# A one-core decoder step: two one-word loads at the start, four token blocks in two transfers, the sample store on another queue

## Chip, core and metric

The kernel runs on one core of a Trainium2 chip. The metric is the device time of one execution in microseconds, as the median of several runs. Engines are called as the profile calls them or by their names: PE or TensorE (matrix products), DVE or VectorE, ACT or ScalarE, POOL or GpSimd, SP or SyncE (which here issues loads and stores).

## The reference

One inference step of a decoder trunk with two parallel head groups: 1024 new prompt tokens and 32 sample tokens (8 sequences of 4), model width 1024, all in float32.

```python
h = rmsnorm(x, norm_g)
proj = h @ w_in                       # 1024 -> 3584: q, f, i (V), za, glu, zb
...
o_a, s_new = hgrn2_chunked(q, k, v, logf, s0)
o_a = rmsnorm(o_a, a_norm_g) * silu(za)
u = glu[..., :B] * sigmoid(glu[..., B:])
cv, buf_new = causal_dwconv(u, conv_buf, conv_w, conv_b)
o_b = silu(layernorm(cv, ln_g, ln_b)) * silu(zb)
out = concat([o_a, o_b]) @ w_out
...
y = rmsnorm(x + out, final_norm_g)    # prompt and sample tokens
```

The outputs are y for both kinds of tokens and the new recurrent and convolution states.

## The kernel before

Tokens lie in nine blocks: eight of 128 prompt tokens (0 to 7) and one of the 32 sample tokens (8). `program` (L1301) emits the kernel twice through `emit`: once in a fast form, then, under a branch on a flag that the fast form has computed, once in a slow form that is safe for extreme inputs. With these inputs the branch is taken over the slow form, so every engine jumps over its instructions at the end.

The start of `emit`. ScalarE loads an activation table (L239). TensorE does 13 products on a constant tile that only keep it busy (`keep(NWARM)`, L245). SP issues the loads in a written order: block 0 (L154), the weights `gin` of the first norm, one row for all 128 partitions (L249), the first of four slices of V's columns of `w_in` (`wi`, L254), block 1, the other three slices, then blocks 2, 8, 3, 4, 5, 6, 7. Blocks 4 to 7 go into `cv`, a tile that is free at that time, one transfer each. After that come the small constants, `cols` (L342) first.

For each block, `stats_x` (L174) has ScalarE square and sum a row, take logarithm and exponential for the root (L176 to L178), and VectorE multiply the block with the root and `gin`. `turn_x` (L193) transposes the block on TensorE, and ScalarE and VectorE split it into a high and a low part. V of blocks 0 and 1 is multiplied slice by slice (`v_part`), with products that only keep TensorE busy in between. `seq` fixes the order of these instructions on each engine as they are written.

Then come 28 blocks of `w_in`'s columns, the recurrence, the convolution and the output product, all woven together by a scheduler. Each load or store carries one of eight completion semaphores in turn (DMAHW0 to DMAHW7), and its issue waits for the transfer that had this semaphore before.

The end. `sample_out` (L1180) follows the last prompt block: TensorE multiplies the 32 sample tokens, VectorE adds the input, ScalarE squares and sums, TensorE adds up over partitions with a matrix of ones (`bones`, L1201), VectorE and ScalarE make the root with one correction step, VectorE multiplies result, root and the final norm's weights `gs` in one instruction, and SP stores it:

```python
V.scalar_tensor_tensor(ys, ys, y, gs, ALU.mult, ALU.mult)
nc.sync.dma_start(h["o_ys"], ys)
```

Behind it `program` loads the flag into a register of every engine (L1305) and branches (L1306); then all engines meet at the barrier that ends the program (L1394).

Of the kernel before, what the change touches and what calls it, by code (L numbers as in the profile page):

```python
# [14 lines left out]
AF = mybir.ActivationFunctionType  # L15
ALU = mybir.AluOpType
AX = mybir.AxisListType

P = 128
D = 1024  # L20
# [12 lines left out]
EPS = 1e-6  # L33
# [20 lines left out]
C_END = C_LOG + 8  # L54
# [43 lines left out]
def emit(nc, tc, h, fast, flag_out=None):  # L98
    HW = 5
    with ExitStack() as ctx:  # L100
# [5 lines left out]
        def sb(shape, tag, bufs=1, dt=F32):  # L106
            return pool.tile(shape, dt, tag=tag, name=tag, bufs=bufs)

        def big(dt=F32, w=TOK):
            return pool.tile([P, 4, w], dt, tag="big", name="big", bufs=6)  # L110

        def bank(tag, bufs):
            return psp.tile([P, 512], F32, tag=tag, name=tag, bufs=bufs)
# [4 lines left out]
        def aux():  # L118
            return bank("aux", 2)

        S = nc.scalar
        V, T = Clock(nc.vector, _dve_ns), Clock(nc.tensor, _pe_ns)
# [17 lines left out]
        gin = sb([P, D], "u", 2)  # L140
        cv = big()
# [4 lines left out]
        X = {"raw": 1, "u": 2, "wh": 2, "qkg": 5}  # L146
        XTAG = ("raw", "u", "wh", "wh", "raw", "qkg", "u", "wh", "qkg")

        def load_x(tb):
            n = P if tb < 8 else ST  # L150

            xr = cv[:, tb - 4, 0:D] if 4 <= tb < 8 else sb([P, D], XTAG[tb], X[XTAG[tb]])
            src = h["xp"][tb * P : (tb + 1) * P, :] if tb < 8 else h["xs"]
            nc.sync.dma_start(xr[0:n, :], src)  # L154
            return xr, n

        def after(ins, prev):
            tc.add_manual_dep(
                getattr(ins, "ins", ins),
                getattr(prev, "ins", prev).name,  # L160
                mybir.DependencyInfo(mybir.DependencyClass.NoSync, mybir.DependencyReason.DATA),
                reason="order of one engine",
            )
# [78 lines left out]
        def keep(n, rhs=av):  # L242

            for _ in range(n):
                seq("P", T.matmul(warm[:, 0:P], lhsT=av, rhs=rhs, start=True, stop=True))  # L245

        keep(NWARM)
        xs = {0: load_x(0)}
        nc.sync.dma_start(gin, h["gin"].partition_broadcast(P))  # L249
        keep(2, gin[:, 0:P])  # L250
        wrs = []
        for j in range(4):
            wr = sb([P, 2, 512], "wraw" if j < 2 else "wl", 2)
            nc.sync.dma_start(wr, h["wi"][:, 2 * j : 2 * j + 2, :])  # L254
            wrs.append(wr)
            if j == 0:
                xs[1] = load_x(1)
        for tb in (2, 8, 3, 4, 5, 6, 7):
            xs[tb] = load_x(tb)


        v01 = [bank("ops", 1), bank("ptps", 1)]
# [75 lines left out]
        S.copy(vs, vps[:, 0:P])  # L338


        cols = sb([P, C_END], "cols")
        nc.sync.dma_start(cols, h["cols"])  # L342
        nmask = 1 if fast else NMASK
        masks = sb([P, nmask, P], "masks", dt=U8)
# [24 lines left out]
        bones = sb([P, P], "bones")  # L369
# [627 lines left out]
        for i, (kind, c) in enumerate(order):  # L997
# [10 lines left out]
            w = ws.pop(0)  # L1008
# [27 lines left out]
            elif kind == "f":  # L1036
# [7 lines left out]
                for hf in range(4):  # L1044
                    gs = g[:, hf * 256 : hf * 256 + 256]
                    V.tensor_tensor_scan(gs, rst, gs, 0.0, ALU.mult, ALU.add)
                gs = g[:, SEQ:TOK]
# [64 lines left out]
        for ko in range(KO):  # L1112
# [17 lines left out]
            ins = S.copy(hi, wr)  # L1130
# [50 lines left out]
        def sample_out(prev):  # L1181
            ys, gs = sio
            ops_s = bank("ops", 1)
            for ko in range(KO):
                for q in range(4):
                    ins = T.matmul(
                        ops_s[q * ST : (q + 1) * ST, 0:256],
                        lhsT=(mixa if ko < 4 else cv)[:, ko % 4, SEQ:TOK],
                        rhs=wraws[ko][:, q * 256 : (q + 1) * 256],
                        start=(ko == 0),  # L1190
                        stop=(ko == KO - 1),
                        tile_position=(0, q * ST),
                    )
                    after(ins, prev)
                    prev = ins
            V.tensor_tensor(ys, ops_s[:, 0:256], ys, ALU.add)
            sq = sb([P, 1], "ss", 4)
            junk = sb([P, 512], "ho", 2)
            S.activation(junk[:, 0:256], ys, AF.Square, accum_out=sq)  # L1199
            sp = aux()  # L1200
            T.matmul(sp[:, 0:1], lhsT=bones, rhs=sq, start=True, stop=True)  # L1201
            y = sb([P, 1], "ss", 4)
            w = sb([P, 1], "ss", 4)

            V.tensor_scalar(w, sp[:, 0:1], -0.5 / D, -0.5 * EPS, ALU.mult, ALU.add)
            S.activation(y, sp[:, 0:1], AF.Ln, bias=eps, scale=1.0 / D)  # L1206
            S.activation(y, y, AF.Exp, scale=-0.5)  # L1207
            V.scalar_tensor_tensor(w, y, y, w, ALU.mult, ALU.mult)
            V.scalar_tensor_tensor(y, w, 1.5, y, ALU.add, ALU.mult)
            V.scalar_tensor_tensor(ys, ys, y, gs, ALU.mult, ALU.mult)  # L1210
            nc.sync.dma_start(h["o_ys"], ys)

        def split_mix(tb):
            ts = slice(tb * P, (tb + 1) * P)
# [10 lines left out]
        def out_mm(ps, mix, half, ko):  # L1225
            hi, lo = mix
            whi, wlo = wo[ko]
            for j, (a, w) in enumerate(
                ((hi, whi[:, half * 512 : half * 512 + 512]), (hi, wlo[half]),
                 (lo, whi[:, half * 512 : half * 512 + 512]))  # L1230
            ):
                ins = T.matmul(
                    ps,
                    lhsT=a[:, ko, :],
                    rhs=w,
                    start=(ko == 0 and j == 0),
                    stop=(ko == KO - 1 and j == 2),
                )
            return ins
# [49 lines left out]
        for tb in range(2, 8):  # L1289
# [3 lines left out]
            for half in range(2):  # L1293
                for ko in range(KO):
                    last = out_mm(ps[half], mix, half, ko)
            finish(tb, ps)
        sample_out(last)


def program(nc, tc, h, fallback=True):  # L1300
    with tc.tile_pool(name="flag", bufs=1) as fp:  # L1301
        flag = fp.tile([1, 1], I32, name="flag")
        emit(nc, tc, h, True, flag)
        if fallback:
            slow = nc.values_load(flag[0:1, 0:1], min_val=0, max_val=1)  # L1305
            with tc.If(slow > 0):  # L1306
                emit(nc, tc, h, False)

# [97 lines left out]
```

## Time and profile before

| | |
|---|---|
| median of 3 runs | 488.61 us (488.42 to 488.77) |
| profiled execution | 488.44 us |
| its span, first to last instruction | 486.7 us |
| TensorE busy | 477.5 us (98% of the span) |
| VectorE busy | 353.7 us (73%) |
| ScalarE busy | 258.3 us (53%) |
| mean granted TensorE clock | 0.994 |
| moved by DMA | 43.78 MB |

The profile is of one execution. Busy time counts an engine's instructions, but not loads of registers, branches, semaphore waits or the issuing of transfers. The time outside the span, 1.7 us here, is in the device time and not in the profile.

### The profile page before, as it was taken

What the parts mean: (1) busy time and instruction counts of PE and PEld (TensorE: products, weight loads), DVE (VectorE), ACT (ScalarE), POOL (GpSimd) and SP (SyncE); (2) the same over time, 40 slices, a digit from 0 to 9 for tenths busy, and PEclk for the clock granted to TensorE, in tenths of its full rate; (3) what the DMA queues carried; (4) which work ended last, traced back from release to release, by engine and by line L of the source; (5) the groups of instructions that cost most, each with busy time, mean ns of one, the idle gap of its engine ahead of it and who ended that gap; (6) DMA issues with size and microseconds to landing.
All of it is one profiled execution on the core that took longest, in us unless ns stands there. A gap on an engine that the chain in (4) does not pass through costs nothing.

```text
span 486.7 us, 7566 instructions
## 1 busy us (share of the span) xinstructions
PE 477.5 (98%) x2970; PEld 445.7 (92%) x2970; DVE 353.7 (73%) x670; ACT 258.3 (53%) x481; POOL 3.0 (1%) x20
## 2 busy tenths in 40 slices
PE   8999999999999999999999999999999999999993
PEld 7788899999999999999999999999999988888881
DVE  4764313999999988999699999995587767334322
ACT  5764322422686564563656547464877876333322
POOL 1000000000000000000000000000000000000000
PEclk9999999999999999999999999999999999999997
DMA  7910501221111202231121211131115289233111
GB/s 268 332 45 13 179 0 48 52 54 44 43 45 43 55 7 65 85 97 43 44 66 45 88 45 48 50 129 46 45 50 172 78 302 386 79 114 145 43 44 61
DMA packets 23628, 43.78 MB, mean 90 GB/s; under 512 B 10881, under 2 KB 12673, under 8 KB 23457
## 3 DMA queue, kind: packets, MB, share of 16 engines
q1 hardware_dynamic: 22432, 41.13, 26.1%
q10 hardware_dynamic: 1152, 2.10, 1.1%
q8 instruction: 25, 0.41, 0.3%
q14 instruction: 19, 0.15, 0.1%
HBM read 35.72 MB, written 7.24 MB: 88 GB/s over the span
## 4 chain that ended last, share of the span: by engine, by line
PE 97%; DMA 1%; DVE 0%; ACT 0%; issue 0%; SPq 0%
PE mm L73 77%; PE ops L73 9%; PE ptps L73 7%; PE aux L73 5%; DMA u<-gin 1%; DVE ho L73 0%; DVE ss L73 0%; ACT ho L1199 0%; SPq L154 0%; ACT ss L1206 0%; ACT ss L1207 0%
## 5 line engine op out<-in xcount | busy, mean ns | idle before, releaser
L73 PE MATMUL mm<-big,wh 128*128 128x352 f32 (+1 forms) x1280 | 324.0, 332 | 0.0
L73 PEld LDWEIGHTS mm<-big,wh 128*128 128x128 f32 x1280 | 224.2, 188 | 6.7 <-issue 0.6
L73 PE MATMUL mm<-big,wl 128*128 128x352 f32 (+1 forms) x640 | 211.3, 330 | 0.0
L73 PEld LDWEIGHTS mm<-big,wl 128*128 128x128 f32 x640 | 120.5, 188 | 3.2
L73 DVE TENSOR_TENSOR wl<-wraw,wh 128x1024 fp32r<-128x1024 f32 x24 | 29.3, 1219 | 23.3 <-ACT wh L412 23.3
L73 DVE SCALAR_TENSOR_TENSOR big<-u,wsum,big 128x511 f32<-128x511 f32 (+14 forms) x60 | 44.3, 738 | 0.5
L73 DVE SCALAR_TENSOR_TENSOR big<-u,cols,big 128x511 f32<-128x511 f32 (+14 forms) x60 | 44.0, 735 | 0.0
L73 DVE SCALAR_TENSOR_TENSOR cq<-u,cols,cq 128x511 f32<-128x511 f32 (+13 forms) x56 | 41.1, 735 | 0.1
L73 DVE TENSOR_TENSOR qkg<-mm,big 128x512 f32<-128x512 f32 x16 | 11.0, 690 | 36.0 <-PE mm L73 28.7
L412 ACT CAST wh<-wraw 128x1024 fp32r<-128x1024 f32 x24 | 25.2, 1049 | 17.4 <-issue 7.8
L1259 ACT ACTIVATE big<-qkg 128x512 f32<-128x512 f32 x16 | 10.1, 631 | 35.8 <-DVE qkg L73 32.9
L417 ACT ACT_TABLE_LOAD x20 | 25.7, 1283 | 0.3
L480 ACT ACTIVATE qkg<-mm 128x352 f32<-128x352 f32 x48 | 19.4, 466 | 11.4 <-PE mm L73 11.3
L73 PE MATMUL mm<-vt,wh 128*128 128x512 f32 x64 | 25.0, 391 | 0.0
L73 PE MATMUL mm<-vt,wl 128*128 128x512 f32 x64 | 24.8, 390 | 0.0
L73 PE MATMUL ops<-big 128*128 128x512 f32 (+1 forms) x96 | 22.7, 395 | 0.0
L73 PE MATMUL ptps<-big 128*128 128x512 f32 x64 | 20.2, 396 | 0.0
L480 ACT ACT_TABLE_LOAD x15 | 19.2, 1283 | 0.3
L554 ACT ACTIVATE hw<-qkg,rng 128x128 f32<-128x128 f32 x32 | 10.2, 393 | 13.5 <-PE ops L73 13.5
L910 ACT ACTIVATE u<-mm,cols 128x352 f32<-128x352 f32 (+2 forms) x16 | 6.5, 485 | 17.7 <-PE mm L73 17.7
L73 PE MATMUL mm<-hw,wh 128*128 128x512 f32 x40 | 15.6, 389 | 0.0
L73 PEld LDWEIGHTS ops<-big 128*128 128x128 f32 (+1 forms) x96 | 12.6, 162 | 3.1 <-ACT big L284 0.2
(237 smaller groups left out, 637.1 us busy)
## 6 DMA issues: line engine op xcount, KB each, us to landing
wraw<-win SPq DMA_DIRECT2D x24, 512.0 KB, 3.6
wraw<-wo SPq DMA_DIRECT2D x8, 512.0 KB, 4.0
big<-xp SPq DMA_DIRECT2D x2, 2048.0 KB, 8.9
big<-xp SPq DMA_DIRECT2D x4, 512.0 KB, 11.1
raw<-sh SPq DMA_DIRECT2D x4, 512.0 KB, 3.4
o_hs<-raw SPq DMA_DIRECT2D x4, 512.0 KB, 2.9
o_yp<-qkg SPq DMA_DIRECT2D x8, 256.0 KB, 3.4
o_yp<-qkg ACTq DMA_DIRECT2D x8, 256.0 KB, 3.6
```

The costliest lines, as they stand in the source:

```text
L73: return f(*a, **k)
L412: S.copy(hi, wr)
L417: after(S.preload_act_table_set("natural_log_exp_and_others"), prev)
L480: return [S.activation(dst[:, nb * MB : (nb + 1) * MB], ps, func, bias=bias)]
L554: S.activation(kb[:, cs], gv[:, cs], AF.Exp, bias=r0[:, cc : cc + 1], scale=-1.0)
L910: out.append(S.activation(dst, src, func, bias=bias))
L1259: S.activation(xr[:, hs], y[:, hs], AF.Square, accum_out=sqs[:, half : half + 1])
```

## The change

At the start ScalarE's queue issues two small loads behind its table load: one word of `wi` per partition, and one word of `gin` for all partitions. They go into two columns of the tile `cols`, which the real load of `cols` overwrites later. Blocks 4 and 5, and blocks 6 and 7, are loaded with one transfer each pair. In `sample_out` the product with the final norm's weights is taken before the root is known (`gs` becomes the result), the last instruction multiplies with the root alone, the flag's register loads are put at fixed places ahead of the end, and ScalarE's queue issues the store.

```diff
         xs = {0: load_x(0)}
+
+        cols = sb([P, C_END], "cols")
+        nc.scalar.dma_start(cols[:, 0:1], h["wi"][:, 0, 0:1])
+        nc.scalar.dma_start(cols[:, 1:2], h["gin"][0:1].partition_broadcast(P))
         nc.sync.dma_start(gin, h["gin"].partition_broadcast(P))
...
-        for tb in (2, 8, 3, 4, 5, 6, 7):
+        for tb in (2, 8, 3):
             xs[tb] = load_x(tb)
+        for tb in (4, 6):
+
+            nc.sync.dma_start(
+                cv[:, tb - 4 : tb - 2, 0:D],
+                h["xp"][tb * P : (tb + 2) * P, :].rearrange("(k p) d -> p k d", p=P),
+            )
+            xs[tb] = cv[:, tb - 4, 0:D], P
+            xs[tb + 1] = cv[:, tb - 3, 0:D], P
...
             S.activation(junk[:, 0:256], ys, AF.Square, accum_out=sq)
+            V.tensor_tensor(gs, ys, gs, ALU.mult)
...
+                loads, (slow,) = nc.values_load_multi_w_load_instructions(
+                    flag_out, min_val=0, max_val=1
+                )
+                loads = {i.ins.engine: i for i in loads}
+                after(loads[nc.vector.engine], half)
+                after(loads[S.engine], root)
+                after(loads[nc.tensor.engine], tot)
+            ins = V.scalar_tensor_tensor(w, y, y, w, ALU.mult, ALU.mult)
+            if flag_out is not None:
+                after(ins, loads[nc.vector.engine])
             V.scalar_tensor_tensor(y, w, 1.5, y, ALU.add, ALU.mult)
-            V.scalar_tensor_tensor(ys, ys, y, gs, ALU.mult, ALU.mult)
-            nc.sync.dma_start(h["o_ys"], ys)
+            V.tensor_scalar(gs, gs, y, None, ALU.mult)
+
+            ins = nc.scalar.dma_start(h["o_ys"], gs)
+            if flag_out is not None:
+                after(ins, loads[S.engine])
+            return slow
```

`half`, `root` and `tot` are the step on the row sums on VectorE, the exponential on ScalarE and the product with `bones` on TensorE. Three places show how instructions move.

SP's queue at the start, before (`raw`, `u`, `wh`, `qkg` and `big` are the tiles that blocks 0, 1, 2 and 3, 8, and 4 to 7 are loaded into; the semaphores that an issue waits for stand in brackets):

```order
L154 DMA raw<-xp 128x1024
L249 DMA u<-gin 128x1024
L254 DMA wraw<-wi 128x1024
L154 DMA u<-xp 128x1024
L254 DMA wraw<-wi 128x1024
L254 DMA wl<-wi 128x1024 x2
L154 DMA wh<-xp 128x1024
L154 DMA qkg<-xs 32x1024 [waits DMAHW0_49]
L154 DMA wh<-xp 128x1024 [waits DMAHW1_49]
L154 DMA big<-xp 128x1024 [waits DMAHW2_49]
L154 DMA big<-xp 128x1024 [waits DMAHW3_49]
```

and with the change, from the second slice of V's weights on:

```order
L257 DMA wraw<-wi 128x1024
L257 DMA wl<-wi 128x1024
L257 DMA wl<-wi 128x1024 [waits DMAHW0_49]
L153 DMA wh<-xp 128x1024 [waits DMAHW1_49]
L153 DMA qkg<-xs 32x1024 [waits DMAHW2_49]
L153 DMA wh<-xp 128x1024 [waits DMAHW3_49]
L265 DMA big<-xp 128x2x1024 [waits DMAHW4_49]
L265 DMA big<-xp 128x2x1024 [waits DMAHW5_49]
L352 DMA cols<-cols 128x153 [waits DMAHW6_49]
```

The two word loads on ScalarE's queue take the second and third semaphore of the eight, so that V's last slice now waits for block 0 and block 2 for the first word, where before neither waited.

ScalarE's queue at the end, before (the last store of the prompt, the steps on the sample tokens, the flag's load, the branch):

```order
L1274 DMA o_yp<-qkg 128x512 [waits Activation_49]
L1199 ACTIVATE ho,ss<-ho 128x256 [waits DVE_49]
L1206 ACTIVATE ss<-aux,eps 128x1 [waits DVE_49]
L1207 ACTIVATE ss<-ss 128x1 [waits Activation_49]
L1305 TENSOR_LOAD flag [waits DVE_49]
L1306 COMPARE_AND_BRANCH
```

and with the change:

```order
L1301 DMA o_yp<-qkg 128x512 [waits Activation_49]
L1209 ACTIVATE ho,ss<-ho 128x256 [waits DVE_49]
L1217 ACTIVATE ss<-aux,eps 128x1 [waits DVE_49]
L1218 ACTIVATE ss<-ss 128x1 [waits Activation_49]
L1222 TENSOR_LOAD flag [waits DVE_49]
L1235 DMA o_ys<-rst 128x256 [waits DVE_49]
L1332 COMPARE_AND_BRANCH
```

The store stands between ScalarE's flag load and its branch; on SP, whose flag load stands far ahead, the branch now follows the last store of the prompt.

VectorE at the end, the piece of the difference between both programs (`ho` holds the sample tokens, `rst` the final norm's weights, `ss` the one-column values):

```order
 L73 TENSOR_TENSOR ho<-ops,ho 128x256
+L73 TENSOR_TENSOR rst<-ho,rst 128x256
 L73 TENSOR_SCALAR ss<-aux 128x1
+L1222 TENSOR_LOAD flag
 L73 SCALAR_TENSOR_TENSOR ss<-ss 128x1 x2
-L73 SCALAR_TENSOR_TENSOR ho<-ho,ss,rst 128x256
-L1305 TENSOR_LOAD flag
-L1306 COMPARE_AND_BRANCH
+L73 TENSOR_SCALAR rst<-rst,ss 128x256
+L1332 COMPARE_AND_BRANCH
```

VectorE's flag load moves from behind its last product to ahead of the correction step, and one product of 256 columns is added ahead of the step on the row sums.

## Rows read from the trace of the kernel before

**Rows 1.** The page, part 4: the chain that ended last, by line.
```profile
PE mm L73 77%; PE ops L73 9%; PE ptps L73 7%; PE aux L73 5%; DMA u<-gin 1%; DVE ho L73 0%; DVE ss L73 0%; ACT ho L1199 0%; SPq L154 0%; ACT ss L1206 0%; ACT ss L1207 0%
```

**Rows 2.** Timeline, 0 to 26 us: start, us, engine, line, operation [idle before <-releaser].
```profile
4.34 1.06 ACT L176 ACTIVATE hw<-raw 128x1024 bf16<-128x1024 f32 x1 [2.32 <-DMA raw<-xp]
...
5.85 0.20 ACT L178 ACTIVATE ss<-ss 128x1 f32<-128x1 f32 x1
...
6.92 1.41 DVE L73 SCALAR_TENSOR_TENSOR raw<-raw,ss,u 128x512 f32<-128x512 f32 x2 [5.34 <-DMA u<-gin]
...
8.38 4.94 SPq L154 DMA_DIRECT2D big<-xp  x4
...
9.82 1.06 ACT L176 ACTIVATE hw<-u 128x1024 bf16<-128x1024 f32 x1 [0.16 <-DMA u<-xp]
...
25.86 1.10 ACT L176 ACTIVATE hw<-big 128x1024 bf16<-128x1024 f32 x1
```

**Rows 3.** The chain in order of time: start, us, what.
```profile
1.19 5.59 DMA u<-gin
```

**Rows 4.** Windows: busy us (instructions) of PE, PEld, DVE, ACT, POOL; granted clock, DMA share, GB/s.
```profile
5.00:6.00 1.00, 1.00 (x7) 1.00 (x7) 0.00 (x0) 0.94 (x4) 0.00 (x0) 1.00 0.74 225
8.00:9.00 1.00, 1.00 (x10) 0.77 (x8) 0.95 (x2) 0.56 (x1) 0.00 (x0) 1.00 1.02 414
```

**Rows 5.** Timeline, 478 us to the end.
```profile
478.31 0.33 SPq L1278 DMA_DIRECT2D o_yp<-qkg  x1
...
480.09 0.16 DVE L73 TENSOR_SCALAR ss<-aux 128x1 f32<-128x1 f32 x1 [1.01 <-PE aux L73]
...
480.81 0.41 DVE L73 SCALAR_TENSOR_TENSOR ss<-ss 128x1 f32<-128x1 f32 x2 [0.56 <-ACT ss L1207]
481.26 0.48 DVE L73 SCALAR_TENSOR_TENSOR ho<-ho,ss,rst 128x256 f32<-128x256 f32 x1
481.77 0.33 SPq L1211 DMA_DIRECT2D o_ys<-ho  x1
```

**Rows 6.** DMA issues of the kernel: tiles, queue, count, KB each, us from issue to landing.
```profile
big<-xp SPq DMA_DIRECT2D x4, 512.0 KB, 11.1
...
qkg<-gfin SPq DMA_DIRECT2D x1, 512.0 KB, 4.3
u<-sc SPq DMA_DIRECT2D x4, 120.0 KB, 2.7
...
o_ys<-ho SPq DMA_DIRECT2D x1, 128.0 KB, 1.9
```

**Rows 7.** Instructions of L1306, the branch and what follows it.
```profile
L1306 SPq EVENT_SEMAPHORE  x8: 17/17/17, 484.7 to 485.3; - x8
...
L1306 PEldq COMPARE_BRANCH  x1: 3378/3378/3378, 480.5 to 480.5; - x1
L1306 ACTq COMPARE_BRANCH  x1: 54/54/54, 481.1 to 481.1; - x1
L1306 DVEq COMPARE_BRANCH  x1: 72/72/72, 481.9 to 481.9; - x1
L1306 SPq COMPARE_BRANCH  x1: 45/45/45, 482.2 to 482.2; - x1
L1306 ACTq EVENT_SEMAPHORE  x1: 17/17/17, 483.7 to 483.7; - x1
...
L1306 DVEq EVENT_SEMAPHORE  x1: 21/21/21, 485.0 to 485.0; - x1
```

**Rows 8.** Instructions of L1394, the barrier at the end.
```profile
L1394 SPq DRAIN  x3: 7/7/13, 485.9 to 486.2; - x3
```

**Rows 9.** DMA issues in the stretch 349.8 to 349.9 us, the first load of `wo`.
```profile
wraw<-wo SPq DMA_DIRECT2D x1, 512.0 KB, 3.8
```

**Rows 10.** DMA issues in the stretch 356 to 356.2 us, the second load of `wo`.
```profile
wraw<-wo SPq DMA_DIRECT2D x1, 512.0 KB, 3.6
```

**Rows 11.** Instructions of L1305, flag loads: queue, count, ns min/median/max, first and last start.
```profile
L1305 DVEq TENSOR_LOAD <-flag x1: 542/542/542, 481.3 to 481.3; - x1
```

More of the change, by code (lines that the diff above doesn't have):

```diff
@@ L150, in load_x @@
             n = P if tb < 8 else ST
-            xr = cv[:, tb - 4, 0:D] if 4 <= tb < 8 else sb([P, D], XTAG[tb], X[XTAG[tb]])
+            xr = sb([P, D], XTAG[tb], X[XTAG[tb]])
             src = h["xp"][tb * P : (tb + 1) * P, :] if tb < 8 else h["xs"]
@@ L338, in emit @@
         S.copy(vs, vps[:, 0:P])
-        cols = sb([P, C_END], "cols")
         nc.sync.dma_start(cols, h["cols"])
@@ L1199, in sample_out @@
             S.activation(junk[:, 0:256], ys, AF.Square, accum_out=sq)
+            V.tensor_tensor(gs, ys, gs, ALU.mult)
             sp = aux()
-            T.matmul(sp[:, 0:1], lhsT=bones, rhs=sq, start=True, stop=True)
+            tot = T.matmul(sp[:, 0:1], lhsT=bones, rhs=sq, start=True, stop=True)
             y = sb([P, 1], "ss", 4)
             w = sb([P, 1], "ss", 4)
-            V.tensor_scalar(w, sp[:, 0:1], -0.5 / D, -0.5 * EPS, ALU.mult, ALU.add)
+            half = V.tensor_scalar(w, sp[:, 0:1], -0.5 / D, -0.5 * EPS, ALU.mult, ALU.add)
             S.activation(y, sp[:, 0:1], AF.Ln, bias=eps, scale=1.0 / D)
-            S.activation(y, y, AF.Exp, scale=-0.5)
-            V.scalar_tensor_tensor(w, y, y, w, ALU.mult, ALU.mult)
-            V.scalar_tensor_tensor(y, w, 1.5, y, ALU.add, ALU.mult)
-            V.scalar_tensor_tensor(ys, ys, y, gs, ALU.mult, ALU.mult)
-            nc.sync.dma_start(h["o_ys"], ys)
+            root = S.activation(y, y, AF.Exp, scale=-0.5)
+            slow = None
+            if flag_out is not None:
[9 more added lines that the diff above has]
+                after(ins, loads[nc.vector.engine])
+            V.scalar_tensor_tensor(y, w, 1.5, y, ALU.add, ALU.mult)
+            V.tensor_scalar(gs, gs, y, None, ALU.mult)
+            ins = nc.scalar.dma_start(h["o_ys"], gs)
+            if flag_out is not None:
+                after(ins, loads[S.engine])
+            return slow
         def split_mix(tb):
@@ L1296, in emit @@
             finish(tb, ps)
-        sample_out(last)
+        return sample_out(last)
 def program(nc, tc, h, fallback=True):
@@ L1302, in program @@
         flag = fp.tile([1, 1], I32, name="flag")
-        emit(nc, tc, h, True, flag)
+        slow = emit(nc, tc, h, True, flag[0:1, 0:1])
         if fallback:
-            slow = nc.values_load(flag[0:1, 0:1], min_val=0, max_val=1)
             with tc.If(slow > 0):
```

## The prediction, made before the changed kernel ran

> **What bounds the kernel now.** I read the page first, for the chain that ended last: TensorE holds almost all of it, the load of the norm's weights `gin` holds 1% near the front, and a few short VectorE and ScalarE steps close it [rows 1]. So what the change touches can only matter in two places: ahead of TensorE's unbroken stretch (the first 12 us or so), and behind its last product (from 478.7 us on).
>
> The front, from the timeline: ScalarE starts block 0's statistics when block 0 lands, at 4.34, and ends them at 6.05; VectorE's first product with `gin` starts at 6.92, having waited 5.34 us for `gin` [rows 2]. `gin` was issued at 1.19 and takes 5.59 us [rows 3], so it lands at 6.8. That is 2.5 us after block 0, for 512 KB. At the 414 GB/s of the stretch 8 to 9 us, 512 KB are 1.3 us; in the stretch 5 to 6 us the DMA engines are busy 0.74 of the time and move 225 GB/s [rows 4]. So some 1.2 us are lost around `gin` and the first slice of V's weights. How much of it the path feels is bounded by the statistics: between 6.05 and 6.92 lie 0.87 us, of which 0.1 is the step from the landing to VectorE's start, so at most 0.75 us. Block 1 is awaited too (0.16 us before ScalarE's start at 9.82 [rows 2]), so the later loads must come earlier as well for the whole 0.75.
>
> The tail: VectorE's last product ends at 481.74, SP issues the store until 482.1 [rows 5], the store lands 1.9 us after its issue [rows 6], at 483.7. Yet the span ends at 486.7. The instructions on the line of the branch over the fallback (L1306) say why: every engine jumps over a large piece of program, and stands still after it. ScalarE branches at 481.1 and does its next instruction at 483.7 (2.6 us later), SP 482.2 and 484.7 (2.5), VectorE 481.9 and 485.0 (3.1), TensorE's branch itself lasts 3.38 from 480.5 [rows 7]. SP is last to branch, since the store waits for the last product. After it SP clears eight load semaphores one by one (484.7 to 485.3 [rows 7]), then as many other ones, and reaches its first drain at 485.9 [rows 8], a walk of 1.2 us; from there to the end are 0.8 us. So **SP's jump sets the end**, not the store's landing.
>
> **Part 1, the two word loads.** They are two issues on ScalarE's queue, where ScalarE has nothing to do before 4.34 (it waits 2.32 us for block 0 [rows 2]); each costs some 0.33 us of issue, by SP's at 481.77 [rows 5], hidden there. Their 256 pieces of 4 bytes share the DMA engines with block 0 and `gin`. The nearest row for their price is the load `u<-sc`, 1024 pieces of 120 bytes, which lands in 2.7 us all told [rows 6]: a quarter of it, 0.7 us, bounds what 256 pieces can hold up. Block 0 may be late by that much at no cost, since the statistics have 0.87 us to spare; `gin` may not.
>
> What can they give? If the loss around `gin` is that of tensors read for the first time, up to 0.75 us; if it has another cause, nothing. Two rows bear on it. The first load of `wo` takes 3.8 us, the second 3.6 [rows 9, 10]: a fresh tensor costs 0.2. The load of `gfin`, one row read 128 times like `gin`, takes 4.3 [rows 6], 0.7 over the second `wo` (it may owe some of that to a larger load ahead of it): reading one row for all partitions may be slow in itself, and a word read before would not change that. I take **0.2 us gained**, by the row of the fresh tensor, and keep 0.75 gained and 0.7 lost as the ends.
>
> A third cause is load, and the rows speak against it: `gin`'s stretch moves 225 GB/s and the later one 414 [rows 4]. The Trainium skill (HBM Reference, section Latency) has an access at 0.2 us on average and at 2 us under high load; by that rule `gin` would be late for the traffic around it and the words would give nothing, 487.45 in place of my sum. The trace disagrees so far as it goes, since the late stretch is the emptier one.
>
> Eight completion semaphores go round among the loads, and a load waits for the one eight before it. Two more loads shift this: V's last slice now waits for block 0, block 2 for the first word. Issue moves by 0.7 us or so; these transfers stand in a queue that takes some 10 us (11.1 for blocks 4 to 7 [rows 6]), so I cost it at nothing. Without that cover it would be those 0.7.
>
> **Part 2, blocks 4 to 7 in two transfers.** Two issues fewer on SP, the same bytes in the same order. Block 4 now counts as landed with block 5. It was issued at 8.38 [rows 2] and landed 11.1 later, at 19.5; its pair is 1.3 us more, 20.8. ScalarE first reads block 4 at 25.86 [rows 2]. 5 us cover it: **0**. Were the cover gone, it would be 1.3 us.
>
> **Part 3, the tail.** Four edits, one path.
> - The product with the final norm's weights moves ahead, into the time in which VectorE waits 1.01 us for TensorE's row sums: at most the 0.48 of the present last product, hidden [rows 5]. The last product becomes one operand shorter. I leave it at 0.48 [rows 5]; it can only shrink, to some 0.3, which would give up to 0.2 us.
> - VectorE's load of the flag moves between its 480.09 step and the product at 480.81. It takes 0.54 [rows 11]; from 480.10 it ends at 480.64, and VectorE waits for ScalarE's root until 480.81 in any case [rows 5]. **0**; the cover is 0.17 us.
> - VectorE then branches with its last product's issue, at some 481.3 and not 481.9, and is through at 484.4 with its 3.1 us.
> - The store goes to ScalarE's queue: issue from 481.77 to 482.1, landing at 483.7 or a little later. ScalarE branches behind it, and with its 2.6 us is through at 484.7. SP branches after its last store of the prompt, issued from 478.31 to 478.64 [rows 5], is through at 481.3, waits for the store's landing (483.7), and does the rest, half of its walk of 1.2 us, by 484.3. TensorE is through at 483.9 [rows 7], as before.
>
> The last to reach the barrier is then ScalarE, at some 484.75, where SP came at 485.9. The end follows 0.8 us later, at 485.55 in place of 486.7: **1.15 us gained**.
>
> The Trainium skill says (DMA: Bandwidth & Descriptors, section Issuing engines are not separate DMA queues) that loads and stores of all engines run on the same DMA engines, and that issuing from several only saves the issuing engine's time. By that rule alone the move is worth the 0.33 us of SP's issue, and the time is 488.3. The trace does not agree here: no transfer sets the end, and what the store holds back on SP is the jump and the walk of 1.2 us behind it, which ScalarE does not have.
>
> **The sum.** 1.15 + 0.2 = 1.35 us less. The profiled execution took 488.44 (span 486.7); that gives 487.1. The median of the runs, 488.61, lies 0.17 above it; the forecast for the median is **487.25 us**.
>
> **Rivals.**
> - *The loss at the front goes whole* (the words open what made both `gin` and V's weights slow): 0.75 in place of 0.2, 486.7 us. For it: the emptiest stretch of the loads is just there. Against: the second `wo` is only 0.2 faster than the first [rows 9, 10], and the load of `gfin` late in the kernel is slow as well.
> - *ScalarE's jump is as long as VectorE's* (3.1 us, the store now being moved in the same time) and the words give nothing: barrier at 485.25, end at 486.05, 0.6 gained, 488.0 us. For it: TensorE's branch lasts even longer, 3.4 us [rows 7]. Against: ScalarE's and SP's are alike, 2.6 and 2.5.
> - *The store's move saves SP's issue alone*: 0.33 us, 488.3. It needs another engine that comes to the barrier at 485.6 whatever SP does; no row shows one. It is what the rule on issuing engines above gives.
> - *The words hold up `gin`* by the 0.7 of their bound: tail less front, 488.15 us.
> - *Slower*: `gin` is late by far more than the words' own pieces, because they and block 0 open three tensors at once. The place is VectorE's first product. When `gin` lands after 8.0 the tail's gain is spent; from 8.9 on the kernel is measurably slower. If it falls as far behind again as it is behind block 0 now (2.5 us, landing at 9.3), the time is 489.95. For it: nothing but the position of the words ahead of everything. Against: 256 pieces have 0.7 us as their bound.
>
> That the change does not do what it says can be for the words: if ScalarE's table load, at the front of its queue, holds their issue back by its 1.3 us, `gin`'s word comes with `gin`. That ends at 487.45.
>
> **How the numbers follow.** A difference of 0.2%, 1.0 us, is about what a measurement of this kernel can tell. Forecast 0.42 (with the case in which the words give nothing, 487.45), front whole 0.33, longer jump 0.08, issue alone 0.04, `gin` held up 0.08, slower 0.05. Faster by over 0.2% means below 487.6: the front-whole case, and the forecast's but for some 0.05 of its end: 0.70. Within 0.2%: the three small cases, and that rest: 0.25. Slower: 0.05. The range goes from 486.4 (front whole, and a shorter last product) to 488.3 (the longer jump, or `gin` held up); it leaves out the slower case and the edges.
>
> **What would show it.** Right: VectorE's first product still waits for `gin`, ended at 6.6 or so; SP's branch near 478.7; flag loads of VectorE and ScalarE ahead of the store; ScalarE's first instruction behind its branch near 484.7, and the first drains of all engines done by 484.8; blocks 4 to 7 awaited by nobody. Wrong: a VectorE idle time ended by the flag load, ScalarE through its jump after 485.5, or VectorE's first product later than 6.92.

## The result and the profile after

The changed kernel takes **489.61 us** (median of 14 runs, 489.38 to 490.50) against 488.47 for the kernel before (14 runs on the same chip): a ratio of 1.0024, 95% interval 1.0017 to 1.0031. It is 1.1 us slower, where 1.35 us faster was forecast. The profiled execution took 489.58, its span 487.8.

Three places have changed. **The front** is later. From the timeline of the changed kernel, 0 to 11 us (columns as in [rows 2]):

```profile
0.77 0.39 ACTq L250 DMA_DIRECT2D cols<-wi  x1
...
1.19 0.45 ACTq L251 DMA_DIRECT2D cols<-gin  x1
...
4.54 1.06 ACT L175 ACTIVATE hw<-raw 128x1024 bf16<-128x1024 f32 x1 [2.52 <-DMA raw<-xp]
...
7.59 0.71 PE L73 MATMUL mm<-u,st 128*128 128x128 f32 x4 [1.76 <-DMA u<-gin]
7.68 1.41 DVE L73 SCALAR_TENSOR_TENSOR raw<-raw,ss,u 128x512 f32<-128x512 f32 x2 [6.11 <-DMA u<-gin]
...
9.47 0.69 DVE L73 CAST big<-wraw 128x1024 fp32r<-128x1024 f32 x1 [0.38 <-DMA wraw<-wi]
```

The words were issued at 0.77 and 1.19, beside ScalarE's table load and not behind it. VectorE's first product with `gin` starts at 7.68, not 6.92 [rows 2], and its next step now waits for V's weights too. The DMA issues of 0.5 to 2.2 us (tiles, queue, count, KB each, us to landing) say what each load took:

```profile
raw<-xp SPq DMA_DIRECT2D x1, 512.0 KB, 3.8
u<-gin SPq DMA_DIRECT2D x1, 512.0 KB, 6.4
wraw<-wi SPq DMA_DIRECT2D x1, 512.0 KB, 7.8
...
cols<-wi ACTq DMA_DIRECT2D x1, 0.5 KB, 3.9
cols<-gin ACTq DMA_DIRECT2D x1, 0.5 KB, 6.8
```

`gin` takes 6.4 us where it took 5.59 [rows 3], and the word of `gin`, 512 bytes in all, takes 6.8. While both are awaited, the DMA engines have little to do (windows, columns as in [rows 4]):

```profile
5.00:6.00 1.00, 0.82 (x8) 0.63 (x6) 0.00 (x0) 0.97 (x3) 0.00 (x0) 1.00 0.29 115
6.00:7.00 1.00, 0.00 (x0) 0.00 (x0) 0.00 (x0) 0.22 (x2) 0.00 (x0) 1.00 0.27 99
7.00:8.00 1.00, 0.41 (x3) 0.41 (x4) 0.32 (x1) 0.00 (x0) 0.00 (x0) 1.00 0.78 283
8.00:9.00 1.00, 0.76 (x7) 0.53 (x5) 1.00 (x2) 0.00 (x0) 0.00 (x0) 1.00 1.03 422
```

From 5 to 7 us they are busy less than 0.3 of the time; in 5 to 6 us it was 0.74 before [rows 4].

**The last stretch**, which the change was not expected to touch, is longer. I measure it from the first product of `hw` with `wh` to VectorE's sum on the sample tokens. Timeline of the kernel before:

```profile
387.01 0.40 PE L73 MATMUL mm<-hw,wh 128*128 128x512 f32 x1
...
478.65 0.42 DVE L73 TENSOR_TENSOR ho<-ops,ho 128x256 f32<-128x256 f32 x1 [0.38 <-PE ops L73]
```

and of the changed kernel:

```profile
388.18 0.39 PE L73 MATMUL mm<-hw,wh 128*128 128x512 f32 x1
...
480.74 0.42 DVE L73 TENSOR_TENSOR ho<-ops,ho 128x256 f32<-128x256 f32 x1 [0.38 <-PE ops L73]
```

That is 91.64 us before and 92.56 after: 0.92 us more, with no wait in it and a granted clock of 1.00. It grows evenly, by some 0.1 us in every 10.

**The tail** gains: from that sum to the end 8.05 us before (486.7 less 478.65), 7.06 now. The instructions of the branch in the changed kernel (laid out as in [rows 7]):

```profile
L1332 SPq EVENT_SEMAPHORE  x8: 17/17/17, 484.5 to 486.1; - x8
...
L1332 SPq COMPARE_BRANCH  x1: 45/45/45, 480.8 to 480.8; - x1
...
L1332 DVEq COMPARE_BRANCH  x1: 72/72/72, 483.5 to 483.5; - x1
L1332 ACTq COMPARE_BRANCH  x1: 54/54/54, 484.2 to 484.2; - x1
...
L1332 DVEq EVENT_SEMAPHORE  x1: 21/21/21, 486.4 to 486.4; - x1
L1332 ACTq EVENT_SEMAPHORE  x1: 17/17/17, 486.9 to 486.9; - x1
```

SP now branches at 480.8, ahead of the store, and has done its eight waits by 486.1; ScalarE is the last to be through, at 486.9.

So, of the profiles: front and middle +1.17 us (387.01 to 388.18), last stretch +0.92, tail -0.99, together +1.10.

### The profile page after: what moved, and what is told of

Read it like the earlier page. It is cut to its first block, busy times and chain, and to the rows that moved or that the text cites. A ratio compares the mean times of both kernels' runs of the same rounds, so it can differ in the third digit from the quotient of the medians.

```text
span 487.8 us, 7565 instructions
## 1 busy us (share of the span) xinstructions
PE 477.7 (98%) x2970; PEld 445.2 (91%) x2970; DVE 353.9 (73%) x671; ACT 258.1 (53%) x481; POOL 3.0 (1%) x20
## 4 chain that ended last, share of the span: by engine, by line
PE 97%; DMA 2%; DVE 0%; SPq 0%; issue 0%; DVEq 0%; ACT 0%
PE mm L73 77%; PE ops L73 8%; PE ptps L73 7%; PE aux L73 5%; DMA wraw<-wi 2%; DVE big L73 0%; DVE ss L73 0%; ACT ho L1209 0%; DVEq L1222 0%; DVE ho L73 0%; SPq L252 0%; SPq L153 0%; DVE rst L73 0%; DVEq L73 0%
```

## The experiments

All were timed against the kernel before, whose median was 488.47 to 488.56 in all of them. "Front" is the start of VectorE's first product with `gin`, "stretch" the time from the first `hw` product to the sum on the sample tokens. Of the theories that are said below to hold, many missed their own range of times by 0.03 to 0.39 us (e1 to e7, e13, e16, e17); the readings rest on differences between runs and on traces.

| | median us | against | front | stretch |
|---|---|---|---|---|
| before | 488.5 | | 6.92 | 91.64 |
| changed | 489.61 | before +1.14 | 7.68 | 92.56 |
| e1 tail alone | 487.73 | before -0.78 | | 91.65 |
| e2 words alone | 490.70 | before +2.19 | 7.73 | 92.57 |
| e3 change without words, `cols` in its old place | 487.77 | before -0.74 | 6.71 | 91.65 |
| e4 as e3, `cols` at the start | 488.69 | e3 +0.92 | 6.75 | 92.57 |
| e5 as e4, word of `gin` | 490.09 | e4 +1.40 | 7.83 | 92.56 |
| e6 as e4, word of `wi` | 488.83 | e4 +0.14 | 6.92 | |
| e7 as e4, tiles moved by 1024 bytes | 487.51 | e4 -1.18 | | 91.65 |
| e8 as e3, tiles moved by 512 | 487.64 | e3 -0.13 | 6.90 | 91.65 |
| e9 as e7, word of `gfin` | 487.97 | e7 +0.46 | 7.56 | |
| e10 as e7, 128 words of `gin` | 488.29 | e7 +0.78 | 7.34 | |
| e11 as e3, store on SP | 488.59 | e3 +0.82 | | |
| e12 as e3, `gin` one row, spread by TensorE | 490.03 | e3 +2.26 | 6.84 | |
| e13 as e3, `gin` 128 rows in memory | 486.65 | e3 -1.12 | 6.05 | 91.65 |
| e14 as e13, both words, tiles moved by 1024 | 486.85 | e13 +0.20 | 6.34 | |
| e15 as e3, tiles moved by 256 | 487.76 | e3 -0.01 | | 91.65 |
| e16 as e3, both operands moved by 128 | 487.14 | e3 -0.63 | 6.72 | 91.25 |
| e17 the change, tiles moved by 1024 | 488.46 | changed -1.15 | 7.53 | 91.65 |
| e18 e13 and e16 together | 486.46 | before -2.08 | 6.17 | 91.24 |

### The parts apart (e1 to e4)

e1 takes the tail's edits alone; e2 the two words alone, with the early `cols` that they need; e3 is the change without the words:

```diff
-        cols = sb([P, C_END], "cols")
-        nc.scalar.dma_start(cols[:, 0:1], h["wi"][:, 0, 0:1])
-        nc.scalar.dma_start(cols[:, 1:2], h["gin"][0:1].partition_broadcast(P))
...
+        cols = sb([P, C_END], "cols")
         nc.sync.dma_start(cols, h["cols"])
```

and e4 drops the two loads only, and leaves the allocation of `cols` at the start.

> The kernel before with the tail's edits alone (no words, four single transfers). Theory W (the two word loads cost about 1.0 us at the front and are also behind the slower output products of the last stretch; the tail gives about 1.0 us back): about 1.0 us faster than before, 487.3 to 487.6, TensorE's last stretch as before (389 to 477 us in 86.5 us, not 87.4), front as before (first VectorE product at 6.9). Rival P (the last stretch is slower because of the tail's own edits, such as the changed order of loads of the flag or another place of tiles): end about as before, 488.2 to 488.6, with the last stretch at 87.4 us. Rival V (the last stretch varies from run to run): 487.4 in the median, and the stretch may be either.

> The kernel before with the two word loads alone. Theory W: slower than before by the front (0.9 to 1.1 us) and the last stretch (0.9 us), together 489.4 to 490.5, first VectorE product at 7.6 or later. Rival M (the merged transfers of blocks 4 to 7 cause the front's delay or the slow last stretch): front as before, or 489.4 without the slow stretch. Rival P: front later by 1.0 and last stretch as before, 489.4.

> The changed kernel without the two word loads, the tile cols allocated where it was before. Theory W: front and last stretch as before, tail as after: 487.3 to 487.6, the same as the tail alone. Rival M: the front is late (first VectorE product at 7.6) or the last stretch slow all the same, 488.4 or more.

> The changed kernel without the two word loads, but with the tile cols still allocated at the start, as the words needed it (it leaves out the words only, and no part of the result). Theory W: as without the words, 487.3 to 487.6. Rival A (the early tile moves other tiles to other addresses, and that makes the last stretch of output products slower by 0.9 us): 488.2 to 488.5, with the first VectorE product at 6.9 and the last stretch at 87.4 us.

e1 and e3 agree at 487.73 and 487.77, so the tail is worth 0.74 to 0.78 us and the merged transfers nothing. e2 is slower by 2.19 (ratio 1.0041, interval 1.0028 to 1.0055). e4 was the surprise: it issues the same loads as e3, and takes 0.92 us longer (no run of one reaches a run of the other), all of it in the last stretch. Rival A holds: **the early tile itself costs 0.92 us**. It moves `wraw`, `wl`, `wh`, `qkg`, `ss` and `hw` by 640 bytes; `big`, `vt` and `cq` stay. Timeline of e3,

```profile
386.88 0.40 PE L73 MATMUL mm<-hw,wh 128*128 128x512 f32 x1
...
478.53 0.42 DVE L73 TENSOR_TENSOR ho<-ops,ho 128x256 f32<-128x256 f32 x1 [0.38 <-PE ops L73]
```

and of e4:

```profile
386.98 0.39 PE L73 MATMUL mm<-hw,wh 128*128 128x512 f32 x1
...
479.55 0.42 DVE L73 TENSOR_TENSOR ho<-ops,ho 128x256 f32<-128x256 f32 x1 [0.38 <-PE ops L73]
```

91.65 us against 92.57. The groups of TensorE in the stretch 392 to 472 us (count, busy us, mean ns of one) show it in the single product (`wh` and `wl` are the weights, the other tile is streamed past them), in e3

```profile
L73 PE MATMUL mm<-big,wh 128*128 128x512 f32 x121 | 38.0, 393 | 0.0
L73 PE MATMUL mm<-big,wl 128*128 128x512 f32 x60 | 23.2, 389 | 0.0
...
L73 PE MATMUL mm<-vt,wh 128*128 128x512 f32 x56 | 21.8, 390 | 0.0
L73 PE MATMUL mm<-hw,wh 128*128 128x512 f32 x35 | 13.6, 389 | 0.0
```

and in e4:

```profile
L73 PE MATMUL mm<-big,wh 128*128 128x512 f32 x120 | 37.6, 393 | 0.0
L73 PE MATMUL mm<-big,wl 128*128 128x512 f32 x60 | 23.5, 395 | 0.0
...
L73 PE MATMUL mm<-vt,wh 128*128 128x512 f32 x55 | 21.7, 395 | 0.0
L73 PE MATMUL mm<-hw,wh 128*128 128x512 f32 x35 | 13.8, 394 | 0.0
```

Three of the seven groups take 5 or 6 ns more, those of `big` with `wh` take as long as before, and those of `cq` with `wh`, few in number, take less (399 and 392).

With 0.92 us for the place and another 0.92 for the loads (489.61 less 488.69; the spans of the two profiles differ by 1.1), less 0.74 for the tail, the change comes to +1.10; measured +1.14. That these add up is no check, since each is a step from one kernel to the next; e17 below is one. e2 lies 0.35 over the same two losses, because its end differs: SP's jump takes 3.0 us there, where it takes 2.5 before [rows 7].

### Which word (e5, e6)

e5 drops the line of `wi`'s word, e6 that of `gin`'s; both keep `cols` at the start.

> The changed kernel with the word of gin alone (no word of wi; the tile cols at the start, as in the change, so the run to compare with is the one without words at 488.69). Theory G (the one-word load for all partitions from one address is what holds up gin): 489.4 to 489.7, first VectorE product at 7.6. Theory I (the word of wi is what holds up gin): 488.6 to 488.8, first VectorE product at 6.9. Theory B (each costs its share by its number of pieces): 489.0 to 489.3.

> The changed kernel with the word of wi alone, cols at the start. Theory G: 488.6 to 488.8, or less if the word helps V's weights. Theory I: 489.4 to 489.7, first VectorE product at 7.6. Theory B: 489.0 to 489.3.

Theory G: the word of `wi` costs 0.14 us, which is within the spread of the runs, that of `gin` 1.40. In e5 it is issued first, at 0.77, and block 0 is late as well (5.5 us after the start, not 4.5). Issues of 0.5 to 2.2 us in e5:

```profile
raw<-xp SPq DMA_DIRECT2D x1, 512.0 KB, 4.8
u<-gin SPq DMA_DIRECT2D x1, 512.0 KB, 6.5
...
cols<-gin ACTq DMA_DIRECT2D x1, 0.5 KB, 5.0
```

A part of the 1.40 is TensorE's clock: in e5 TensorE has no product between its 13 filling ones and those that wait for `gin`, and is granted half its clock, 1.2 GHz, afterwards (window of e5):

```profile
8.00:9.00 1.00, 1.00 (x6) 0.91 (x6) 1.00 (x2) 0.00 (x0) 0.00 (x0) 0.50 1.03 422
```

The five runs of e5 go with it: 489.51 us at a mean granted clock of 0.997, 491.07 at 0.993. In the profiled execution of the changed kernel, with a similar gap, the clock stays at 1.00 (above), so the change's own 0.92 has no such part.

### The place of the tiles (e7, e8, e15, e16)

e7 allocates two more small tiles beside the early `cols` (1024 bytes together), e8 moves only `bones` to the start (512), e15 only `rng` (256). e16 puts `masks` (128) ahead of all tiles, so that both operands move:

```diff
+        nmask = 1 if fast else NMASK
+        masks = sb([P, nmask, P], "masks", dt=U8)
         ident = sb([P, P], "ident")
```

> The changed kernel without the words, with cols and two more small tiles (384 bytes) allocated at the start, so that the weight tiles of the output products and the tiles streamed against them move by 1024 bytes and not by 640. Theory O (what costs 0.9 us in the last stretch is the offset of these tiles within 512 bytes against those that do not move): 487.6 to 487.9, as with cols in its old place, and the last stretch in 86.5 us. Rival D (any move away from the old place, or the early allocation itself, costs it): 488.5 to 488.9.

> The changed kernel without the words and with cols in its old place, but with the tile bones (512 bytes) allocated at the start, so that the same tiles move by 512 bytes. Theory O: 487.6 to 487.9, last stretch in 86.5 us. Rival D: 488.5 to 488.9. Rival K (the offset counts within 1024 bytes): this one 488.5 or so, while the move by 1024 bytes is as fast as the old place.

> The changed kernel without the words and cols in its old place, with the tile rng (256 bytes) allocated at the start, so that the same tiles move by 256 bytes. Theory O (any offset but a multiple of 512 bytes): 488.4 to 488.8, last stretch 0.7 to 1.1 us longer. Rival E (offsets of 256 bytes are as good as 512): 487.5 to 487.9.

> The kernel of e3 (487.77) with the tile masks (128 bytes) allocated first of all, so that the tiles streamed in the output products and the tiles loaded as weights all move by 128 bytes together (a few small tiles and cq stay). Theory REL (the place of one operand against the other decides): 487.4 to 488.0, 91.65 us from the first product of hw to the sample tokens' sum, as in e3. Theory ABS (the weights' own place decides, or that of any operand): 488.3 to 488.9, 92.4 us or more.

Moves by 256, 512 and 1024 bytes cost nothing (91.65 us each); the move by 640 costs 0.92. So rival D is out: neither the early allocation nor any move costs it. In e15 theory O's 512 fails and its rival E holds. A step of 256 fits all four, but 640 is the only move tried that is no multiple of it. In e16 weights and streamed tiles moved by 128 together give 91.25 us,

```profile
386.73 0.39 PE L73 MATMUL mm<-hw,wh 128*128 128x512 f32 x1
...
477.98 0.42 DVE L73 TENSOR_TENSOR ho<-ops,ho 128x256 f32<-128x256 f32 x1 [0.38 <-PE ops L73]
```

so theory ABS fails: the weights lie 512 bytes from where they lie in e4, a distance that costs nothing in e8, and the loss is not there. Theory REL, **the place of one operand against the other**, is nearer, but it is not shown. By it e16 would take 91.65 us as e3 does, and it takes 0.4 less, most of it in products whose two operands moved together (group of e16 in the stretch 392 to 472 us; 393 ns in e3):

```profile
L73 PE MATMUL mm<-big,wh 128*128 128x512 f32 x122 | 37.9, 390 | 0.0
```

And in e4 the products of `hw` with `wh`, both moved by 640, grew by 5 ns, while those of `big` with `wh`, of which `wh` alone moved, did not. That the place of the tiles costs the 0.92 is shown; which place against which is open.

### One place read by all partitions (e9, e10, e13, e14)

e9 and e10 add one small load to e7: a word of `gfin` for all partitions, and 128 different words of `gin`. e13 changes nothing in the kernel's order, only where `gin` is read:

```diff
-        nc.sync.dma_start(gin, h["gin"].partition_broadcast(P))
+        nc.sync.dma_start(gin, h["gin"])
...
-        "gin": c(np.asarray(i["norm_in_g"]).reshape(D)),
+        "gin": c(np.repeat(np.asarray(i["norm_in_g"]).reshape(1, D), P, 0)),
```

e14 is e17 with that, and both words from separate rows. In e13, e14 and e18 `gin` lies in memory 128 times, as the input that `gs` is loaded from is repeated already; that layout lies outside the measured time.

> The kernel of e7 (487.51) with one small load added on ScalarE's queue: one word of gfin, a tensor that nobody else reads at that time, for all partitions. Theory S (128 pieces that read one and the same address hold up the loads around them, whatever the tensor): block 0 lands at 5.2 to 5.6, gin at 7.4 or later, 488.4 to 489.2. Theory R (the harm comes from reading the same row as gin's own load at the same time): gin as without words (6.6 to 6.8), 487.4 to 487.8. Theory N (any 128 small pieces do it): as S, but the word of wi alone cost only 0.14, so it is not expected.

> The kernel of e7 (487.51) with one small load added: 128 different words of gin, one per partition, so 128 pieces from 512 bytes of the same tensor. Theory S: these are 128 addresses, so little harm, 487.4 to 487.9. Theory R: harm as with the one word, 488.4 to 489.2, gin at 7.4 or later.

> The kernel of e3 (487.77), same instructions in the same order, but gin lies in memory 128 times, one row for each partition, and is loaded from there. Theory Z (reading one row for all partitions is what makes gin late): gin lands at 5.5 to 5.9 in place of 6.6 to 6.8, VectorE's first product starts at 6.1 to 6.2 (then bound by the statistics), 486.8 to 487.2. Rival C (whatever comes second in the queue is late): gin at 6.5 or later, 487.5 to 488.0.

> The changed kernel with both words, the tiles moved by 1024 bytes as in e7, and gin 128 times in memory: both words are now read from 128 separate rows. Theory Z: harmless like the word of wi alone, within 0.3 of e13. Rival H (a second word costs 0.9 us whatever it reads, for being 128 more pieces ahead of gin's): 0.7 or more above e13.

e9 and e10 fall between the theories. Both delay block 0 (5.1 and 4.6 us after its issue, 3.6 in e3), so a tensor of its own does not protect (against R), nor do 128 addresses in 512 bytes (against S): it is a narrow place. The word of `wi`, also 128 pieces and also first on its queue, but from places far apart, leaves block 0 at 3.8 (e6). In e9 VectorE's first product then waits for the statistics of the late block 0 and not for `gin`. e13 is clear. Issues of 0.5 to 2.2 us in e3,

```profile
raw<-xp SPq DMA_DIRECT2D x1, 512.0 KB, 3.6
u<-gin SPq DMA_DIRECT2D x1, 512.0 KB, 5.4
wraw<-wi SPq DMA_DIRECT2D x1, 512.0 KB, 6.6
```

and in e13:

```profile
raw<-xp SPq DMA_DIRECT2D x1, 512.0 KB, 3.5
u<-gin SPq DMA_DIRECT2D x1, 512.0 KB, 4.4
wraw<-wi SPq DMA_DIRECT2D x1, 512.0 KB, 5.3
```

The same bytes from 128 rows land 1.0 us sooner, the loads behind them 1.3, and the gap in the DMA engines' work is gone (window and timeline of e13):

```profile
5.00:6.00 1.00, 1.00 (x7) 1.00 (x7) 0.00 (x0) 0.94 (x4) 0.00 (x0) 1.00 1.01 410
```

```profile
6.05 1.42 DVE L73 SCALAR_TENSOR_TENSOR raw<-raw,ss,u 128x512 f32<-128x512 f32 x2 [4.47 <-ACT ss L177]
```

VectorE's wait ahead of its first product is then ended by the statistics and no longer by `gin`. e14 puts both words back, from 128 rows, and loses 0.20 us, within the spread of the runs, not 0.7 or more. Theory Z holds: what stalls the loads is that 128 pieces are read from one narrow place, in `gin`'s own load (some 1 us, in the kernel before too) and in the word (0.9 us more). What in the memory serves such reads slowly, no run here shows.

### The tail's own mechanism (e11)

```diff
-            ins = nc.scalar.dma_start(h["o_ys"], gs)
-            if flag_out is not None:
-                after(ins, loads[S.engine])
+            nc.sync.dma_start(h["o_ys"], gs)
```

> The changed kernel without the words and with cols in its old place (as e3, 487.77), but the sample store stays on SP's queue; the other edits of the tail stay. Theory J (SP's jump and its walk behind the store set the end, and the store's move is what gives the time): 0.6 to 0.9 slower than e3, 488.3 to 488.6, of which the shorter last product keeps 0.1 to 0.2 against the kernel before. Rival X (the earlier product and the earlier flag loads give the time, not the queue): 487.6 to 487.9. Rival Q (the move saves only the issue): about 488.1.

488.59: with the store back on SP the whole gain of the tail is gone (theory J). Instructions of the branch, e11:

```profile
L1328 SPq EVENT_SEMAPHORE  x8: 17/17/17, 484.8 to 485.3; - x8
...
L1328 SPq COMPARE_BRANCH  x1: 45/45/45, 481.9 to 481.9; - x1
L1328 ACTq EVENT_SEMAPHORE  x1: 17/17/17, 484.0 to 484.0; - x1
```

and e3:

```profile
L1330 SPq EVENT_SEMAPHORE  x8: 17/17/17, 482.2 to 484.0; - x8
...
L1330 SPq COMPARE_BRANCH  x1: 45/45/45, 478.6 to 478.6; - x1
...
L1330 ACTq EVENT_SEMAPHORE  x1: 17/17/17, 484.8 to 484.8; - x1
```

In e11 SP walks from 484.8 on, as before; in e3 it has jumped long ago and waits only for the store's landing, and ScalarE is the last to be through. The Trainium skill's rule that the issuing engine saves its issuing time alone (DMA: Bandwidth & Descriptors, Issuing engines are not separate DMA queues) would make the move worth 0.33 us; the two runs differ by 0.82, since here SP's program behind the issue moves with it.

### Versions on these findings (e12, e17, e18)

e12 loads `gin` as one row of 4 KB; TensorE multiplies it with a row of 1/128, VectorE scales it back:

```diff
-        keep(NWARM)
+        keep(6)
...
+            seq("P", T.matmul(gp, lhsT=av[0:1, :], rhs=gin[0:1, hs], start=True, stop=True))
+            seq("V", V.tensor_scalar(gin[:, hs], gp, float(P), None, ALU.mult))
...
+        keep(4)
```

> The kernel of e3 (487.77) with gin loaded as one row of 4 KB, and spread over the partitions by two TensorE products with a constant, two VectorE steps scaling them back; the load of gin for 128 partitions is gone, and 9 of the 15 products at the start that only keep TensorE busy. Theory L (the front is bound by the loads: gin's 128 reads of one row cost 1.2 us or more of the queue): wi's first slice lands about 1.2 earlier, at 7.0 to 7.3, VectorE's first product with gin at 6.1 to 6.5 in place of 6.9, 486.8 to 487.3. Rival C (what is lost at the front is the start of the queues, and any tensor that comes second loses it): first slice at 8.0 or later, 487.5 to 488.0. The order of later work is set anew by the scheduler here, which may move the time by some tenths in either direction.

> The whole change with both words, the tiles moved by 1024 bytes and not by 640. If the loss by the place of the tiles (0.92) and that by the words (0.92) add: 488.5 to 488.9, the last stretch as before and gin as late as with the change (7.4 or later). If they are one cause: 487.5 to 487.9 or 489.4 to 489.8.

> The kernel of e16 (487.14) with gin 128 times in memory as in e13. If the two causes are separate, the gains add: 1.1 less than e16, 485.9 to 486.2. If gin's early landing is worth less here: up to 486.7.

e12 missed both ranges: 490.03, its runs spread from 488.45 to 490.78. The loads came sooner as theory L has it (V's first slice 4.5 us after an issue at 1.19), but the two scaling steps of 0.69 us and TensorE's single-row products took the time back: VectorE's first product starts at 6.84, and in the profiled execution TensorE's clock is halved behind it (window of e12):

```profile
8.00:10.00 2.00, 2.00 (x10) 1.82 (x9) 1.54 (x3) 1.13 (x3) 0.00 (x0) 0.50 1.01 342
```

That execution took 488.65, though, and it and the one of 488.45 have the lowest mean clock of the eight, 0.992; the six slower ones have 0.995 to 0.997. So the halved clock does not explain the median, and what the slower ones lose stands in no trace. The edit keeps 10 of the 15 products that only keep TensorE busy, not the 6 that the expectation counts.

e17 shows that the two losses add: with the tiles moved by 1024 the whole change is 1.15 faster than as it was made, and stands level with the kernel before (ratio 0.9999, 0.9990 to 1.0008); the words cost 0.95 there (e17 less e7), about as much as in the change. e18, `gin` from 128 rows and both operands moved, is the fastest at 486.46 (ratio 0.9957, 0.9944 to 0.9971). It lies 0.68 under e16, clear of its runs, and 0.19 under e13, which 5 runs each do not tell apart. That the two gains add in full is not shown: by the medians e18 would be at 486.0, and it came out in the range expected for the case that the early `gin` is worth less here. The spans of the profiles, 485.7 (e3), 485.2 (e13), 485.2 (e16) and 484.7 (e18), do add, but each is of one execution.

## Why the prediction was wrong

- **The words (part 1): the step that failed.** The prediction took 0.2 us gained, with 0.7 lost as the worst, by the number of pieces of `u<-sc`. They cost 0.92 (changed less e4), and the sign of being wrong that it named came: VectorE's first product starts at 7.68, later than 6.92. The count of pieces was the wrong measure: the word of `wi`, 128 pieces too, costs 0.14 (e6), and both words from separate rows 0.20 (e14). What decides is where they are read. The rival "the words hold up `gin`" had the right place and sign; it was given 0.08.
- The prediction weighed [rows 6] rightly and then dropped them: the slow load of `gfin` said that one row read by all partitions may be slow in itself. e13 shows this for `gin`. So a first reading of fresh tensors, the reason for the 0.2, was not the cause of the gap at all; nor was load, the cause that the prediction rejected.
- **The early `cols`: a term that was missing.** The description of the change names the tile, and the prediction priced nothing for its new place. It costs 0.92 us, some 390 us behind the code that was changed (e4). No row of the trace before could price it; but the address of every tile behind an early allocation changes, and that was there to be read in the diff.
- **The tail (part 3): right, but too large.** 1.15 forecast; 0.74 to 0.78 in the medians of e1 and e3 (0.90 and 1.03 in those of e8 and e7, which have the same tail), 0.99 in the profile of the change. The sizes that were off: ScalarE stood still for 2.8 us behind its branch (482.0 to 484.8 in e3), not 2.6, and from its first instruction to the end of the span are 0.9 us, not 0.8. Two more cancel: VectorE's flag load took 0.65 us where the prediction put 0.54 [rows 11], so it outlasted its cover by 0.11, and the last product fell to 0.35 us, which gave 0.13 back. That ScalarE was forecast through at 484.75 and is at 484.8 in e3 is partly luck: e3 comes to the sum on the sample tokens 0.12 earlier than the kernel before. That SP's jump set the end is shown by e11.
- **Merged transfers: 0**, as forecast (e1 and e3 differ by 0.04). The shift of the semaphores comes with the words and was not run alone; e14 has it too, and loses 0.20 at most. That the words would be held back by the table load did not happen: they were issued at 0.77 and 1.19.
- The sum, by these terms: +0.92 +0.92 -0.74 = +1.10 in place of -1.35.

## What to carry to other kernels

In this kernel a load that every partition reads from one row, and a small load that all partitions read from one narrow place, were slow and held up the loads beside them; try such a vector laid out once per partition if it stands at the head of a kernel. A tile that is allocated earlier moves all tiles behind it: look at how far, and compare the per-product time of TensorE's long stretches before and after. Where engines end with a jump and a barrier, ask which engine jumps last, and give the last store to one with little to do behind it.

## What the runs showed of the hardware

- 512 KB read as 128 times one row land 1.0 us later than from 128 rows (5.4 and 4.4 us after the issue, e3 and e13), and the loads behind them 1.3 later.
- Products of 128x128 weights with 512 columns took 0.92 us more in 91.65 (1%) when the tiles of their weights and some of the streamed ones were moved by 640 bytes against the rest, and nothing more for 256, 512 or 1024 (e3, e4, e7, e8, e15). The Trainium skill (SBUF — State Buffer, section Who interferes with whom) gives TensorE independent ports for the weights and for what streams past them; by that alone I would not expect their places to matter. The runs show that places matter by some 1%, not whether these ports are the reason.
- The jump over the slow form stands ScalarE, SP, VectorE and TensorE still for 2.5 to 4.4 us (4.4 is TensorE's in e15), GpSimd for only 0.5. It is not the same for one engine in two kernels: SP's took 2.5 us before [rows 7], 2.9 in e11 and 3.6 in e3. The Trainium skill (Runtime: NRT & Kernel Launch, section Instruction fetch mechanics) has a taken branch out of the loaded window wait for a fetch of its target; the stall in the runs agrees with it, and the fetch itself is in no trace.
